# A hybrid attention block: the fourth query tile is turned in two transfers, and the rotary queries and mask biases are asked for at another place

## The chip, the cores and the metric

The kernel runs on one core of a Trainium2 chip. A core has the matrix engine PE (its weight loads, PEld, overlap its products), the vector engine DVE, the scalar engine ACT, the general engine POOL, and SP, which here computes nothing: it issues every DMA of the kernel, in one order, one after another. The metric is the time of one execution in microseconds (us). Three runs of the kernel before are shown, and beside them one profiled execution whose trace is read here.

## The reference

One decoder block: sixteen meta tokens stand ahead of 512 real ones, so L = 528 rows of width 1024, all in float32. Two attention branches run on one projection of the normalised input, and their gated outputs are added.

```python
u = rmsnorm(h, pre_norm_g)
cq, ckv, k_pe, z_mla, fq, fk, fv, f_logit, z_fox, gate_a, gate_b = split(u @ w_in)
# MLA: 16 heads; 64 plain and 32 rotary dimensions in queries and keys, values of 64
q = rmsnorm(cq) @ w_uq ; kv = rmsnorm(ckv) @ w_ukv
o_mla = causal_softmax_attention([q_nope, rope(q_pe)], [k_nope, rope(k_pe)], v_mla)
y_mla = (o_mla * silu(z_mla)) @ w_br_mla
# FoX: 16 heads of 64; a cumulative log forget gate is added to the scores
cum = cumsum(log_sigmoid(f_logit + b))
o_fox = causal_softmax_attention(fq, fk, fv, bias = cum[t] - cum[s])
y_fox = (o_fox * silu(z_fox)) @ w_br_fox
mixed = (sigmoid(gate_a) * y_mla + sigmoid(gate_b) * y_fox) @ w_out
return (h + rmsnorm(mixed, post_norm_g))[:, 16:]
```

## The kernel before

Products are split: an operand is kept as a high and a low 16-bit part, and one product becomes three (high x high, high x low, low x high), which is why PE does so much.

The attention runs as sixteen stages, `stages = [(br, pr) ...]`: for each pair of heads `pr` = 0..7 first FoX (`br` = 1), then MLA (`br` = 0). They are written (1,4), (0,4) and so on below. The 512 real queries are cut into four query tiles of 128, b = 0..3; tile b sees the meta keys and b+1 blocks of 128 keys, each block as a high and a low part, so 2b+3 tiles of probabilities for each of the two heads: 6, 10, 14 and 18 blocks of 128x128 for b = 0, 1, 2, 3.

One stage does this, each step with the name under which the profile shows it:

- `scores`: PE multiplies queries and keys into `st` (MLA's rotary part uses the tiles `KPH`, `KPL` and `QP`); DVE moves `st` to `sf` and adds a row of `cb` on the way (L1037). `cb` holds the forget-gate biases of the pair: plain ones, `cbp`, two loads of 264 KB by `bias` (L1159), and masked ones, `cbm`, made from them on POOL by `masked_bias`.
- ACT takes the exponential and sums each row into `su` (L1072). `norm(g)` then scales `su` (L1076) and inverts it into `ri` (L1077) in `inverse`, POOL does the meta columns (from L1092), ACT writes the high part of the normalised probabilities (L1107), DVE the low part (L1111), both into `pn`. Group g = 0 holds b = 0, 1, 2 (`pn0`), group 1 holds b = 3 (`pn1`).
- SP issues one DMA transpose for each query tile from `pn` into `ptt` (the profile's "pt<-pn"), at the end of `norm`. `ptt` has 18 blocks by 512 queries; tile b fills the first 2(2b+3) blocks of its own 128 queries.
- `values`: PE runs the 26 matmuls of `ov`: two on the meta block, then for each key block j = 0..3 six of them, which read blocks 2..5, 6..9, 10..13 and 14..17 of `ptt`. Their width shrinks with j: 512, 384, 256 and 128 queries. The two meta matmuls read block 0 and 1 of all four query tiles.

PE's order is written out by hand (`tc.manual_schedule`). Between a stage's scores and its `ov` stand the matmuls that project the next heads (`fq`, `fk`, `v`, `mq`, `mk`, `z`) and, right ahead of `ov`, the scores of the next stage. Each of these needs its weights: SP loads `wraw`, ACT, DVE and POOL (L274, L275) scale and split them into `w`. The order on DVE, ACT, POOL and SP is chosen by a scheduler from the program's order and priorities; `tc.issue_after(x)` adds that what it encloses stands behind x. SP carries all of it in one queue: weights `wraw`, transposes of values `vp<-vh`, biases `cbp`, transposes "pt<-pn", and for the rotary part of MLA's queries the stores to `qpe_dram` and the load `QP<-qpe_dram` of 256 KB. `load_qp` is called in `q_done`, when the pair's query projection has been evicted.

The DMAs use eight semaphores in turn, so that in the order below a DMA that names DMAHWn waits for the eighth one ahead of it, or for one whose bytes it needs. Names such as DVE or PE behind "waits" are the semaphores of the engines.

Of the kernel before, what the change touches and what calls it, by code (L numbers as in the profile page):

```python
# [17 lines left out]
ALU = mybir.AluOpType  # L18
# [8 lines left out]
NH = 16  # L27
# [13 lines left out]
PSCALE = 512.0  # L41
# [15 lines left out]
def block_kernel(ctx: ExitStack, tc: tile.TileContext, x, meta_tokens, pre_norm_g, w_in, fox_forget_b,  # L57
                 mla_q_norm_g, mla_kv_norm_g, w_uq, w_ukv, w_br_mla, w_br_fox, w_out, post_norm_g,
                 rope_tok, rope_pe, out):
    nc = tc.nc  # L60
# [21 lines left out]
    su = const.tile([128, 64], F32, tag="su", name="su")  # L82
# [12 lines left out]
    def dma(out, src, start=None):  # L95

        with tc.issue_after(sums_out[0]) if written[0] and sums_out else nullcontext():
            ins = (start or nc.sync.dma_start)(out=out, in_=src)
        if written[0]:
            tc.keep_in_program_order(ins)  # L100
        return ins.ins
# [683 lines left out]
    with ExitStack() as att:  # L785
# [38 lines left out]
        nc.gpsimd.memset(vh[:, 0], 0.0)  # L824
        for b in range(4):
            nc.gpsimd.memset(pn[b // 3][:, PN_STEP * b % 15], 0.0)
        gT = []
        masks, normed, whole, turned_p, between = [], [], [], [], []

        def load_qp(pr):  # L830
            dma(f32(QP), qpe_dram[2 * pr : 2 * pr + 2].rearrange("h i x f s -> (h i x f) s"))

        def q_mla(pr):
            def cuts(raw):
                return [(raw[:, 0:384].rearrange("p (b e) -> p b e", e=96)[:, :, 0:NOPE], lambda t: t[:, 0:256].rearrange("p (b e) -> p b e", e=NOPE)),
                        (raw[:, 384:640].rearrange("p (h a e) -> p a h e", h=2, a=2), lambda t: t[:, 256:512].rearrange("p (a h e) -> p a h e", a=2, h=2))]

            def wrap(w):
                mw[pr] = w
                return (lambda k: w[k][0]), (lambda k: w[k][1])  # L840
            get = mws[pr] = Parts(lambda: [wuq[:, :, 192 * pr : 192 * pr + 192], wukv[:, 256 * pr : 256 * pr + 256]], mla_room, cuts, wrap)

            halves = hl_done(("q", 0, pr), S, S, get)

            def q_done(i, ps):
                halves(i, ps)
                if pr:
                    load_qp(pr)
            return unit(f"mq{pr}", get, cq_act, 2, REAL, q_done)


# [144 lines left out]
        def attention(br, pr):  # L996
# [76 lines left out]
                                                                scale=-1.0, accum_out=sums["su"][:, h, b : b + 1]).ins  # L1073

            def inverse(su, ri):
                nc.vector.tensor_scalar(out=su, in0=su, scalar1=1.0 / PSCALE, scalar2=None, op0=ALU.mult)  # L1076
                return nc.vector.reciprocal(ri, su).ins  # L1077

            def norm(g):
                def fn():  # L1080
                    b0, nb_ = GRP[g][0], len(GRP[g])
                    su, ri = (sums[t][:, :, b0 : b0 + nb_] for t in ("su", "ri"))
                    if not (three_first and g):
                        inv = inverse(su, ri)
                    if three_first and g == 0:
                        with tc.issue_after(inv):
                            evict([p_ for p_ in places if p_[0] == 3])

                    mt = aw.tile([128, 2, nb_, META], F32, tag=f"mt{g}", name=f"mt{nm_}{g}", bufs=1)
                    src = sfs[g][:, :, 0 : SF_STEP * nb_].rearrange("p h (b c) -> p h b c", b=nb_)[:, :, :, 0:META]  # L1090
                    dst = pn[g][:, 0 : PN_STEP * nb_].rearrange("p (b t) h c -> p h b t c", b=nb_)[:, :, :, 0]
                    nc.gpsimd.tensor_tensor(out=mt, in0=src, in1=ri.unsqueeze(3).broadcast_to([128, 2, nb_, META]),  # L1092
                                            op=ALU.mult)
                    hi, lo, hi2 = (dst[:, :, :, 32 * i : 32 * i + META] for i in range(3))
                    nc.gpsimd.tensor_copy(hi, mt)
                    lead[:] = lead[-1:] + [nc.gpsimd.tensor_tensor(out=lo, in0=mt, in1=hi, op=ALU.subtract).ins]
                    nc.gpsimd.tensor_copy(hi2, mt)
                    def parts(b, h):
                        sf = sf_of(h, b)[:, META:].rearrange("p (j c) -> p j c", c=128)
                        t0 = PN_STEP * (b % 3) + 1  # L1100
                        hi, lo = (pn[g][:, t0 : t0 + 2 * b + 2, h].rearrange("p (j l) c -> p j l c", l=2)[:, :, i]
                                  for i in range(2))
                        return sf, hi, lo, sums["ri"][:, h, b : b + 1]

                    def high(b, h):
                        sf, hi, _, rib = parts(b, h)
                        normed[:] = [nc.scalar.activation(hi, sf, AF.Copy, scale=rib).ins]  # L1107

                    def lower(b, h):
                        sf, hi, lo, rib = parts(b, h)  # L1110
                        nc.vector.scalar_tensor_tensor(out=lo, in0=sf, scalar=rib, in1=hi, op0=ALU.mult, op1=ALU.subtract)  # L1111

                    early = three_first and g == 0
                    for b in GRP[g]:
                        if early and b == GRP[g][-1]:
                            for h in range(2):
                                high(b, h)
                            with tc.issue_after(normed[0]):
                                exponentials((3,))
                            inv = inverse(*(sums[t][:, :, 3:4] for t in ("su", "ri")))  # L1120
                            with tc.issue_after(inv):
                                for h in range(2):
                                    lower(b, h)
                            continue
                        for h in range(2):
                            high(b, h)
                            lower(b, h)
                    for b in GRP[g]:
                        t0, n = PN_STEP * (b % 3), 2 * b + 3
                        turned_p[:] = [dma(ptt[:, 0 : 2 * n, 128 * b : 128 * b + 128], pn[g][:, t0 : t0 + n].rearrange("p t h c -> p (t h c)"),  # L1130
                                           nc.sync.dma_start_transpose)]
                        if between and b == 1:
                            with tc.issue_after(turned_p[0]):
                                between.pop()()
                return fn
# [23 lines left out]
        def bias(pr):  # L1159

            return [nc.sync.dma_start(cb[0][h], c_dram[2 * pr + h : 2 * pr + h + 1].broadcast_to([128, L])).ins
                    for h in range(2)][1:]
# [35 lines left out]
        g = gate_unit(own=True)  # L1198
# [126 lines left out]
        for si, (br, pr) in enumerate(stages):  # L1325
# [4 lines left out]
            if br and si:  # L1330
                latent_first(sets[si - 1][2], halved[("k", 1, pr), 1])
            sc()
            for fn in late:
                fn()
            if si == 0:
# [24 lines left out]
            else:  # L1360
# [10 lines left out]
                if si == 2:  # L1371
                    behind.clear()
                n0()
                if pr and not (br or last):
                    bias(pr + 1)
                if br:
                    sets[si][0].scale()
                for job in middles[si]:
# [410 lines left out]
```

## Time and profile before

| | |
|---|---|
| three runs | 585.48, 585.65, 582.69 us (median 585.48) |
| the profiled execution | 582.32 us, its span 580.5 us |
| granted clock of PE | 0.998 |
| PE busy | 559.7 us, 96% of the span |
| DVE, ACT, POOL busy | 471.0 (81%), 407.5 (70%), 240.3 us (41%) |
| the chain that ended last | PE 74%, DVE 12%, ACT 5%, issue 3%, DMA 3% |
| transposes pt<-pn | 64 (four in each of the sixteen stages) |
| DMA queue q1 | 97.03 MB, 70.1% of 16 engines' span |

"Busy" adds up an engine's instructions; the chain is followed back from the last instruction to what released each one, and says which engine's work lay on the way to the end. An idle stretch of PE is printed with what released it; where that says "issue", the profile shows nothing that the engine waited for, though the program's order may still show a wait. The span is 1.8 us shorter than the execution's own time, and that execution is 0.5% below the median of the three runs.

### The profile page before, as it was taken

What the parts mean: (1) busy time and instruction counts of PE and PEld (TensorE: products, weight loads), DVE (VectorE), ACT (ScalarE), POOL (GpSimd) and SP (SyncE); (2) the same over time, 40 slices, a digit from 0 to 9 for tenths busy, and PEclk for the clock granted to TensorE, in tenths of its full rate; (3) what the DMA queues carried; (4) which work ended last, traced back from release to release, by engine and by line L of the source; (5) the groups of instructions that cost most, each with busy time, mean ns of one, the idle gap of its engine ahead of it and who ended that gap; (6) DMA issues with size and microseconds to landing.
All of it is one profiled execution on the core that took longest, in us unless ns stands there. A gap on an engine that the chain in (4) does not pass through costs nothing.

```text
span 580.5 us, 11367 instructions
## 1 busy us (share of the span) xinstructions
PE 559.7 (96%) x3865; PEld 391.6 (67%) x3865; DVE 471.0 (81%) x1255; ACT 407.5 (70%) x891; POOL 240.3 (41%) x361
## 2 busy tenths in 40 slices
PE   7999979999899999989999999999999999999995
PEld 6888647667567568557566675645776675788884
DVE  5878899887877988887877879879958986478966
ACT  7869679788887887878887988964443463343762
POOL 4422723785783897866847857700000000000000
PEclk9999999999999999999999999999999999999999
DMA  8625789889999697998995984668924230333603
GB/s 286 147 65 152 216 176 280 177 191 250 190 231 202 159 194 144 221 204 163 262 228 119 237 199 121 139 146 278 299 76 109 73 110 6 110 104 108 218 1 145
DMA packets 220026, 97.75 MB, mean 168 GB/s; under 512 B 131352, under 2 KB 209568, under 8 KB 219968
## 3 DMA queue, kind: packets, MB, share of 16 engines
q1 hardware_dynamic: 219968, 97.03, 70.1%
q8 instruction: 30, 0.49, 0.3%
q14 instruction: 28, 0.23, 0.1%
HBM read 62.62 MB, written 4.23 MB: 115 GB/s over the span
## 4 chain that ended last, share of the span: by engine, by line
PE 74%; DVE 12%; ACT 5%; issue 3%; DMA 3%; POOL 1%; SPq 1%; DVEq 0%; ACTq 0%; POOLq 0%
PE z L104 16%; PE pg L104 10%; PE py L104 8%; PE st L104 6%; PE fq L104 6%; PE x L104 6%; PE v L104 6%; PE ov L104 5%; PE fk L104 5%; PE psm L104 2%; PE y L104 2%; PE mq L104 2%; DVE w L272 2%; DVE sc L204 1%; DVE wl L110 1%
## 5 line engine op out<-in xcount | busy, mean ns | idle before, releaser
L104 PEld LDWEIGHTS <-w 128*128 128x128 f16 x1752 | 168.2, 98 | 126.4 <-DVE w L272 2.5
L1072 ACT ACTIVATE sf<-sf,nb 128x272 f32<-128x272 f32 (+3 forms) x128 | 72.7, 569 | 21.2 <-DVE nb L1037 19.6
L104 PE MATMUL z<-hTh,w 128*128 128x512 f16 x256 | 81.6, 379 | 0.3 <-DVE w L272 0.3
L220 POOL TENSOR_SCALAR sc<-sc,su 128x3 f32<-128x3 f32 (+3 forms) x23 | 9.9, 432 | 163.8 <-DVE sc L217 163.8
L275 POOL TENSOR_TENSOR w<-wraw,w 128x1024 f16<-128x1024 f32 x35 | 75.2, 2148 | 2.3
L1111 DVE SCALAR_TENSOR_TENSOR pn<-sf,ri,pn 128x512 f16<-128x512 f32 (+3 forms) x128 | 70.9, 612 | 3.5 <-ACT pn L1107 3.5
L104 PE MATMUL pg<-hTh,w 128*128 128x512 f16 x240 | 72.6, 379 | 0.8 <-DVE w L272 0.8
L1107 ACT ACTIVATE pn<-sf,ri 128x128 f16<-128x128 f32 (+3 forms) x128 | 59.6, 547 | 6.0 <-issue 2.3
L261 ACT ACTIVATE w<-wraw,sc 128x1024 f16<-128x1024 f32 x42 | 47.0, 1142 | 11.3 <-DVE sc L219 9.0
L110 DVE TENSOR_TENSOR wl<-wraw,w 128x512 fp32r<-128x512 f32 (+1 forms) x44 | 38.5, 881 | 12.5 <-PE scale L104 4.4
L104 PE MATMUL z<-hTl,w 128*128 128x512 f16 x128 | 48.5, 379 | 0.0
L274 POOL TENSOR_SCALAR wraw<-wraw,sc 128x1024 f32<-128x1024 f32 x35 | 39.7, 1133 | 15.3 <-ACT w L261 14.5
L104 PE MATMUL pg<-hTl,w 128*128 128x512 f16 x120 | 45.5, 379 | 0.0
L104 PE MATMUL st<-hlk,hlq 64*128 64x240 f32 (+4 forms) x480 | 42.4, 300 | 1.2 <-DVE gT L894 0.9
L104 PE MATMUL fk<-hTh,w 128*128 128x272 f16 (+1 forms) x224 | 40.2, 276 | 0.0
L104 PE MATMUL ov<-pt,vp 128*64 128x512 f16 (+4 forms) x416 | 32.6, 306 | 6.9 <-DMA pt<-pn 3.4
L104 PEld LDWEIGHTS st<-hlk,hlq 64*128 64x128 f32 x480 | 33.6, 186 | 8.2 <-ACT vh L961 1.7
L104 PE MATMUL v<-hTh,w 128*128 128x272 f16 (+1 forms) x224 | 39.1, 276 | 0.0
L202 ACT ACTIVATE junk<-wraw 128x1024 bf16<-128x1024 f32 (+2 forms) x35 | 33.7, 964 | 3.8 <-DMA wraw<-in_w_in_dram 3.5
L104 PEld LDWEIGHTS <-vp 128*64 128x64 f16 (+1 forms) x416 | 22.6, 109 | 19.3 <-issue 11.6
L104 PE MATMUL fq<-hTh,w 128*128 128x512 f16 x112 | 34.5, 380 | 0.0
L1492 ACT CAST w<-wraw 128x512 fp32r<-128x512 f32 x28 | 16.8, 617 | 23.0 <-DVE wraw L1501 18.5
(345 smaller groups left out, 1459.5 us busy)
## 6 DMA issues: line engine op xcount, KB each, us to landing
wraw<-in_w_in_dram SPq DMA_DIRECT2D x46, 512.0 KB
room<-in_w_in_dram SPq DMA_DIRECT2D x9, 512.0 KB
cbp<-c_dram SPq DMA_DIRECT2D x16, 264.0 KB
wraw<-in_w_br_fox_dram SPq DMA_DIRECT2D x8, 512.0 KB
tb<-in_w_out_dram SPq DMA_DIRECT2D x8, 512.0 KB
wraw<-in_w_br_mla_dram SPq DMA_DIRECT2D x8, 512.0 KB
wraw<-in_w_out_dram SPq DMA_DIRECT2D x6, 512.0 KB
QP<-qpe_dram SPq DMA_DIRECT2D x8, 256.0 KB
```

The source lines that it names most:

```text
L104: nc.tensor.matmul(*a, **k)
L110: return eng.tensor_tensor(out=lo, in0=src, in1=f32(hi), op=ALU.subtract)
L202: tc.keep_in_program_order(nc.scalar.activation(junk[0][:, 0:n], raw, AF.Abs, accum_out=mp))
L220: nc.gpsimd.tensor_scalar(out=r, in0=t, scalar1=su[:, 5:6], scalar2=1.0, op0=ALU.mult, op1=ALU.mult)
L261: self.hi = nc.scalar.activation(hi, raw, AF.Copy, scale=self.s).ins
L272: nc.vector.scalar_tensor_tensor(out=lo, in0=raw, scalar=self.s, in1=hi, op0=ALU.mult, op1=ALU.subtract)
L274: nc.gpsimd.tensor_scalar(out=raw, in0=raw, scalar1=self.s, scalar2=1.0, op0=ALU.mult, op1=ALU.mult)
L275: nc.gpsimd.tensor_tensor(out=lo, in0=raw, in1=hi, op=ALU.subtract)
L1072: exps[b // 3] = nc.scalar.activation(sf, sf, AF.Exp, bias=sums["nb"][:, h, b : b + 1], scale=-1.0, accum_out=sums["su"][:, h, b : b + 1]).ins
L1107: normed[:] = [nc.scalar.activation(hi, sf, AF.Copy, scale=rib).ins]
L1111: nc.vector.scalar_tensor_tensor(out=lo, in0=sf, scalar=rib, in1=hi, op0=ALU.mult, op1=ALU.subtract)
L1492: nc.scalar.copy(to[0], src)
```

## The change

Three edits. First, the transpose of query tile b = 3 goes out as two DMAs: tiles 0 to 4 (10 blocks: meta, j = 0, j = 1) and tiles 5 to 8 (8 blocks: j = 2, j = 3). Second, in `inverse` the sums are scaled through a view whose two outer dimensions are exchanged. Third, for pairs 1 to 6 the call `bias(pr + 1)` moves from the MLA stage (0,pr), behind `n0()`, to the FoX stage (1,pr), right behind `sc()`; its second DMA is kept in `biased`, and `load_qp` of the pair is issued behind it.

```diff
@@ load_qp, q_done
-        gT = []
+        gT, biased = [], []
...
                 if pr:
-                    load_qp(pr)
+                    with tc.issue_after(biased[0]) if biased else nullcontext():
+                        load_qp(pr)
+                    biased.clear()
@@ inverse
-                nc.vector.tensor_scalar(out=su, in0=su, scalar1=1.0 / PSCALE, scalar2=None, op0=ALU.mult)
+                su_ = su.rearrange("p h b -> p b h")
+                nc.vector.tensor_scalar(out=su_, in0=su_, scalar1=1.0 / PSCALE, scalar2=None, op0=ALU.mult)
@@ norm
-                        turned_p[:] = [dma(ptt[:, 0 : 2 * n, 128 * b : 128 * b + 128], pn[g][:, t0 : t0 + n].rearrange("p t h c -> p (t h c)"),
-                                           nc.sync.dma_start_transpose)]
+                        for t, m in ((0, 5), (5, 4)) if b == 3 else ((0, n),):
+                            turned_p[:] = [dma(ptt[:, 2 * t : 2 * (t + m), 128 * b : 128 * b + 128],
+                                               pn[g][:, t0 + t : t0 + t + m].rearrange("p t h c -> p (t h c)"), nc.sync.dma_start_transpose)]
@@ the loop over stages
             sc()
+            if br and 1 <= pr < NH // 2 - 1:
+                biased[:] = bias(pr + 1)
...
                 n0()
-                if pr and not (br or last):
-                    bias(pr + 1)
```

On PE, ACT and POOL the order of the instructions is the same in both kernels, and on DVE too, but for the form of the scaling (128x2x3 becomes 128x3x2 where the group has three query tiles; the form 128x2 of the fourth stays). SP's queue changes, and with it what PE waits for.

SP's queue in the FoX stage (1,4), before: the last transpose of stage (0,3), two stores of rotary queries, the load of QP which waits for both of them, weights, the biases, and this stage's transposes of 6, 10, 14 and 18 blocks.

```order
L98 DMA_TRANSPOSE pt<-pn_777 128x14x128 [waits DMAHW2_49,DVE_49]
L98 DMA qpe_dram<-gT_1016 2x16x512 [waits DMAHW3_49,Pool_49]
L98 DMA qpe_dram<-gT_1016 2x16x512 [waits DMAHW4_49,Pool_49]
L98 DMA QP<-qpe_dram 128x512 [waits DMAHW5_49,DMAHW4_49,DMAHW3_49]
L98 DMA wraw_3747<-in_w_in_dram 128x8x128 [waits DMAHW6_49,Pool_49]
L98 DMA_TRANSPOSE vp_782<-vh 128x9x128 [waits DMAHW7_49,DVE_49]
L98 DMA wraw_3749<-in_w_uq_dram 128x2x192 [waits DMAHW0_49,Activation_49,Pool_49]
L98 DMA wraw_3749<-in_w_ukv_dram 128x256 [waits DMAHW1_49]
L98 DMA wraw_4183<-in_w_in_dram 128x8x128 [waits DMAHW2_49,Pool_49]
L1161 DMA cbp_767<-c_dram 128x528 [waits DVE_49]
L1161 DMA cbp_766<-c_dram 128x528 [waits DVE_49]
L98 DMA_TRANSPOSE pt<-pn_777 128x6x128 [waits DVE_49,DMAHW5_49,PE_49,Pool_49]
```

The same stretch of SP's queue after, from the weights behind the stores to the end of the stage's transposes.

```order
L98 DMA wraw_3756<-in_w_in_dram 128x8x128 [waits DMAHW5_49,Pool_49]
L98 DMA_TRANSPOSE vp_782<-vh 128x9x128 [waits DMAHW6_49,DVE_49]
L98 DMA wraw_3758<-in_w_uq_dram 128x2x192 [waits DMAHW7_49,Activation_49,Pool_49]
L98 DMA wraw_3758<-in_w_ukv_dram 128x256 [waits DMAHW0_49]
L98 DMA wraw_4196<-in_w_in_dram 128x8x128 [waits DMAHW1_49,Pool_49]
L1165 DMA cbp_767<-c_dram 128x528 [waits DMAHW2_49,DVE_49]
L1165 DMA cbp_766<-c_dram 128x528 [waits DMAHW3_49,DVE_49]
L98 DMA QP<-qpe_dram 128x512 [waits DMAHW4_49]
L98 DMA_TRANSPOSE pt<-pn_777 128x6x128 [waits DVE_49,DMAHW5_49,PE_49,Pool_49]
L98 DMA_TRANSPOSE pt<-pn_777 128x10x128 [waits DMAHW6_49,DVE_49,PE_49]
L98 DMA_TRANSPOSE pt<-pn_777 128x14x128 [waits DMAHW7_49,DVE_49,PE_49]
L98 DMA_TRANSPOSE pt<-pn_778 128x10x128 [waits DMAHW0_49,DVE_49]
```

The load of QP has moved from ahead of the weights to behind the biases, directly ahead of the stage's transposes; the biases stand where they stood. The transpose of 18 blocks is now one of 10, and one of 8 follows it. The same holds in (1,5). In stages (1,1), (1,2), (1,3) and (1,6) the load of QP comes to the same place behind the biases, from the MLA stage ahead, where it stood directly before the four transposes.

SP's queue in the MLA stage (0,1), before: QP of the next pair, and the four transposes, in which the fourth query tile comes second.

```order
L98 DMA wraw_2373<-in_w_in_dram 128x8x128 [waits DMAHW7_49,Pool_49]
L98 DMA QP<-qpe_dram 128x512 [waits DMAHW1_49,DMAHW0_49,PE_49]
L98 DMA_TRANSPOSE pt<-pn_777 128x6x128 [waits DVE_49,PE_49,Pool_49]
L98 DMA_TRANSPOSE pt<-pn_778 128x18x128 [waits DMAHW2_49,DVE_49,PE_49]
L98 DMA_TRANSPOSE pt<-pn_777 128x10x128 [waits DMAHW3_49,DVE_49]
L98 DMA_TRANSPOSE pt<-pn_777 128x14x128 [waits DMAHW4_49,DVE_49]
```

And after.

```order
L98 DMA wraw_2380<-in_w_in_dram 128x8x128 [waits DMAHW2_49,Pool_49]
L98 DMA_TRANSPOSE pt<-pn_777 128x6x128 [waits DVE_49,DMAHW3_49,PE_49,Pool_49]
L98 DMA_TRANSPOSE pt<-pn_778 128x10x128 [waits DMAHW4_49,DVE_49,PE_49]
L98 DMA_TRANSPOSE pt<-pn_777 128x10x128 [waits DMAHW5_49,DVE_49]
L98 DMA_TRANSPOSE pt<-pn_777 128x14x128 [waits DMAHW6_49,DVE_49,PE_49]
L98 DMA_TRANSPOSE pt<-pn_778 128x8x128 [waits DMAHW7_49,PE_49]
```

Ahead of this stage's transposes no QP stands any more, and the second half of the fourth tile comes last, behind the 14 blocks of the third.

PE at the start of `ov` in stage (1,4), before: behind the last scores, the first weight load waits for four DMAs, the stage's four transposes.

```order
L104 MATMUL st_3653<-KPH,QP 128x400
L104 MATMUL st_3654<-KPH,QP 128x400
L104 MATMUL st_3653<-KPL,QP 128x400
L104 MATMUL st_3654<-KPL,QP 128x400
L104 LDWEIGHTS vp_782 [waits DMAHW5_49,DMAHW6_49,DMAHW0_49,DMAHW7_49]
L104 MATMUL ov_3675<-pt,vp_782 64x512 [waits PE_49]
```

After, the first weight load still waits for four DMAs, now with the 10-block half among them, and the wait for the 8-block half stands fourteen matmuls later, at the first one of j = 2.

```order
L104 LDWEIGHTS vp_782
L104 MATMUL ov_3686<-pt,vp_782 64x384
L104 LDWEIGHTS vp_782
L104 MATMUL ov_3686<-pt,vp_782 64x384
L104 LDWEIGHTS vp_782
L104 MATMUL ov_3686<-pt,vp_782 64x256 [waits DMAHW1_49]
```

One wait of `ov` has become two, the second of them behind the two meta matmuls and the twelve of j = 0 and j = 1.

## The prediction

> **What bounds the kernel now.** I read the page first, for the engine that fills the span and the chain.
>
> ```profile
> span 580.5 us, 11367 instructions
> PE 559.7 (96%) x3865; PEld 391.6 (67%) x3865; DVE 471.0 (81%) x1255; ACT 407.5 (70%) x891; POOL 240.3 (41%) x361
> ...
> PE 74%; DVE 12%; ACT 5%; issue 3%; DMA 3%; POOL 1%; SPq 1%; DVEq 0%; ACTq 0%; POOLq 0%
> ...
> L104 PE MATMUL ov<-pt,vp 128*64 128x512 f16 (+4 forms) x416 | 32.6, 306 | 6.9 <-DMA pt<-pn 3.4
> ```
>
> PE is busy for 559.7 of 580.5 us, so a change that alters no PE work can win only what PE idles. The last row gives the size of the matter: in all sixteen stages together PE idles 6.9 us ahead of `ov`, 1.2% of the span. The change touches just the DMAs for which `ov` waits. The view of waits, for PE, names what ended that idle time, and what ended the idle time of the scores.
>
> ```profile
> PE ov L104 <- DMA pt<-pn: 3.4, 2, 1.8
> PE ov L104 <- issue: 3.1, 2, 2.0
> ...
> PE st L104 <- DVE gT L894: 0.9, 1, 0.9
> ...
> PE ov L104 <- PE st L104: 0.3, 1, 0.3
> ```
>
> Each row is: engine and tile waiting, releaser, total us, times, longest. So `ov` waits visibly in five of sixteen stages. "issue" is no cause; the order shows that the weight load ahead of that `ov` waits for the four transposes. PE's timeline places the five, the idle time in brackets; the row at 189.44 is the wait for L894, the one at 369.48 an `ov` that did not wait, and the one at 252.31 belongs to the `ov` of 251.28, its six matmuls of j = 1.
>
> ```profile
> 87.09 1.22 PE L104 MATMUL ov<-pt,vp 80*64 80x512 f16 x10 [1.82 <-DMA pt<-pn]
> 148.59 1.65 PE L104 MATMUL ov<-pt,vp 80*64 80x512 f16 x16 [1.58 <-DMA pt<-pn]
> 189.44 2.25 PE L104 MATMUL st<-hlk,hlq 64*128 64x272 f32 x29 [0.93 <-DVE gT L894]
> 251.28 2.04 PE L104 MATMUL ov<-pt,vp 80*64 80x512 f16 x26 [1.99 <-issue]
> 252.31 0.63 PE L104 MATMUL ov<-pt,vp 128*64 128x384 f16 x6
> 291.37 1.87 PE L104 MATMUL ov<-pt,vp 80*64 80x512 f16 x20 [1.12 <-issue]
> 330.58 1.65 PE L104 MATMUL ov<-pt,vp 80*64 80x512 f16 x16 [0.25 <-PE st L104]
> 369.48 1.22 PE L104 MATMUL ov<-pt,vp 80*64 80x512 f16 x10
> ```
>
> The stages are (1,0), (0,1), (1,4), (1,5), (1,6) and, for 369.48, (1,7). Their idle times add up to 1.82 + 1.58 + 1.99 + 1.12 + 0.25 = 6.76 us.
>
> **What delays the transposes there.** SP's timeline for (1,4), (1,5), (1,6) and (1,7), and its waits; columns are start, length, what and how many. Rows of one transpose alone stand below the four that they belong to.
>
> ```profile
> 226.32 1.54 SPq L98 DMA_DIRECT2D qpe_dram<-gT  x2
> 232.13 0.35 SPq L98 DMA_DIRECT2D QP<-qpe_dram  x1
> ...
> 236.55 0.38 SPq L98 DMA_DIRECT2D wraw<-in_w_in_dram  x1
> 236.98 1.06 SPq L1161 DMA_DIRECT2D cbp<-c_dram  x2
> 239.90 9.12 SPq L98 DMA_TRANSPOSE pt<-pn  x4
> ...
> 245.29 3.73 SPq L98 DMA_TRANSPOSE pt<-pn  x1
> ...
> 280.08 9.27 SPq L98 DMA_TRANSPOSE pt<-pn  x4
> ...
> 286.05 3.30 SPq L98 DMA_TRANSPOSE pt<-pn  x1
> ...
> 316.92 1.01 SPq L1161 DMA_DIRECT2D cbp<-c_dram  x2
> 320.16 8.43 SPq L98 DMA_TRANSPOSE pt<-pn  x4
> ...
> 359.37 7.83 SPq L98 DMA_TRANSPOSE pt<-pn  x4
> ...
> SPq L98 <- DMA qpe_dram<-gT: 8.6, 2, 4.4
> ```
>
> The stores' issue ends at 227.86, and QP goes out at 232.13: SP stands still for over 4 us until the stores have landed, once in (1,4) and once in (1,5), 8.6 us together. Everything behind in the queue, four weight loads and a transpose of values among it, then comes in one heap ahead of this stage's transposes. The windows show the heap, the DMA share second to last and GB/s last in each row:
>
> ```profile
> 228.00:233.00 5.00, 5.00 (x62) 3.59 (x61) 4.67 (x27) 4.00 (x14) 4.82 (x7) 1.00 0.36 93
> 233.00:252.00 19.00, 17.01 (x124) 9.94 (x124) 17.00 (x59) 16.20 (x38) 16.16 (x19) 1.00 1.09 219
> ...
> 364.40:366.50 2.10, 2.10 (x16) 1.09 (x16) 1.24 (x7) 1.90 (x5) 2.02 (x3) 1.00 1.14 209
> 366.60:369.10 2.50, 2.50 (x42) 2.50 (x42) 2.50 (x10) 1.31 (x4) 2.50 (x3) 1.00 1.04 181
> ```
>
> The DMA engines are at 0.36 while SP stands still, and full (1.09) from then until `ov` starts. The last two rows are the ends of the 14- and 18-block transposes in (1,7): full engines, 181 to 209 GB/s.
>
> **The change part by part.** I go against the profiled execution, 582.32 us, which is 3.16 us under the median of 585.48; the differences are carried over to the median at the end.
>
> *The split.* A block is 128 x 128 x 2 bytes, 32.8 KB, so 8 blocks are 262 KB. `ov` no longer waits for these: at 181 to 209 GB/s that is 1.25 to 1.45 us of transfer taken from in front of it. Its lower end is zero or worse (rival 3). I take 1.25, the faster row, since the engines have to finish the first half as they would the whole. The 8-block half is wanted by j = 2, which starts some 1.4 us after `ov` (252.31 + 0.63 = 252.94 is the end of the last j = 1 matmul, and `ov` started at 251.28; a matmul overlaps the next by some 0.2). Its transfer, 1.25 to 1.45, ends about then, so a second wait of 0 to 0.3 us may be left. On SP the issue of one 18-block transpose takes 3.30 and 3.73 us in the limited stages, as long as the engines are full; two issues of the smallest kind seen, 1209 ns each in the group of pt<-pn, are shorter than that, so SP's sixteen more DMAs cost nothing there.
>
> ```profile
> L98 SPq DMA_TRANSPOSE pt<-pn x64: 1209/1614/3977, 74.5 to 381.9; - x64
> ```
>
> *QP behind the biases.* In (1,4) and (1,5) SP is freed of 4.2 and 4.4 us. The weights behind the stores go out into engines that are 64% idle. What is gained for the transposes is bounded by rows: (1,6) has the same queue without that wait, biases directly ahead, and its four take 8.43 us to issue, 0.7 to 0.8 less than 9.12 and 9.27. Against it stands QP's own load, now directly ahead of the transposes: 256 KB, 1.25 us at 209 GB/s if the engines are full by then, and 0.35 us of SP. In (1,4) the issue fits in the stretch from 238.04 to 239.90 in which SP waits anyway. So for the transposes this part lies between +0.5 (1.25 - 0.75) and -0.8; I take -0.45. In (1,1), (1,2), (1,3), (1,6) QP comes where SP has a stretch as well: in (1,6) from 317.93 to 320.16. What covers it is SP's wait ahead of the first transpose; if that wait were gone, each would cost 0.35 us of SP. What needs QP is late enough: the first scores with QP in (1,4) start at 246.2 (next fence), 8 us behind the biases.
>
> ```profile
> L104 PE MATMUL st<-KPH,QP x10: 271/283/346, 246.2 to 248.8; 64*128 64x272 f32 x2, 64*128 64x240 f32 x2, 64*128 64x144 f32 x2, 64*128 64x288 f32 x2
> ...
> 136.18 0.58 SPq L98 DMA_DIRECT2D QP<-qpe_dram  x1
> 136.87 8.34 SPq L98 DMA_TRANSPOSE pt<-pn  x4
> ```
>
> The last two rows are stage (0,1): there QP leaves from directly ahead of the transposes, which could start 0.69 us earlier.
>
> *The biases.* The order puts their two DMAs at the same place of SP's queue: 0.
>
> *The form of the scaling.* DVE's 32 scalings take 142 to 1658 ns. The long ones are not the reshaped form: the rows below show a 128x2 scaling at 234.52 that ends at 236.18, when POOL's L275 ends (236.15).
>
> ```profile
> 234.52 1.66 DVE L1076 TENSOR_SCALAR su<-su 128x2 f32<-128x2 f32 x1
> ...
> 234.02 2.13 POOL L275 TENSOR_TENSOR w<-wraw,w 128x1024 f16<-128x1024 f32 x1
> ```
>
> The 128x2 form stays as it is, so this is 0; between 142 ns each saved and lost, sixteen of them off PE's path.
>
> *The sum, stage by stage.* (1,4): 1.25 + 0.45 = -1.70 of 1.99. (1,5): the split alone covers the 1.12; I take -1.1. (1,6): its 0.25, I take -0.2. (0,1): split and QP, 1.25 + 0.69, exceed 1.58; but whatever PE wins before 189 us meets the 0.93 us wait for L894, a chain of DVE work that does not follow from `ov`: PE that comes earlier waits longer there. I take -0.2 out of 1.58. (1,0): 1.82 lies before the same wait, 0. Sum: -1.7 - 1.1 - 0.2 - 0.2 = -3.2 us. The ends: 0, if PE's earlier arrival is given back everywhere, and -6.76, if all is won. So 582.32 becomes 579.1, and the median 585.48 becomes 582.3, -0.55%.
>
> **Rivals.** *1. Given back, no change.* DVE has 17.00 busy of 19 us in 233 to 252 and POOL 16.16, so the engines behind PE have about 2 us of room per stage; with QP in front of six FoX stages' transposes at up to 1.25 us of transfer, the first half lands no earlier than the whole did before. For it: the 1.09 share. Against: QP's bytes move in every version, only earlier, and the stall on stores wastes engines. It gives -1 to +1, 585. A change that does not do what it says belongs here too: the order shows the biases not moved at all.
>
> *2. All `ov` waits go.* It needs the L894 wait to follow. For it: the 0.69 us that leave stage (0,1). It gives up to 585.48 - 6.76, 578.7; I put it at 580.
>
> *3. Slower: the two halves do not overlap.* Between the end of the 18-block issue and `ov` lie 291.37 - 289.35 = 2.02 us and 251.28 - 249.02 = 2.26 us. If a second transfer could begin only when the first has landed, it would be 1.21 + 2.02 = 3.2 us behind it; with the first 1.25 earlier and j = 2 1.4 later, `ov` would end 0.6 us later than now. It decides once the halves land more than 2.65 us apart. Over the six FoX stages (1,1) to (1,6), which I count as without room, that is +3.6 us: 589.1, +0.6%. Against it: in (1,7) the four are issued within 7.83 us, and `ov` starts, unwaited, 10.1 us after the first issue began; four in series would need 4 x 3.2 = 12.8.
> The Trainium skill speaks for this rival: its page "DMA: Bandwidth & Descriptors" (Anatomy of one DMA; Rules for kernel authors) gives each DMA about 2.0 us of fixed cost and asks for many small transfers to be merged into a large one. By its fit, as an estimate, 18 blocks would take 3.35 us and 10 and 8 blocks 2.75 + 2.60, 2.0 more in each stage; the overlap in (1,7) does not bear out that the fixed parts add up one behind another.
>
> **How the numbers follow.** Forecast (1.5 to 4.5 us won) 0.50; rival 1, 0.26; rival 2, 0.12; rival 3, 0.12. A measurement here tells about 0.5%, 2.9 us, from no change. The forecast's own range is 581 to 584; its centre of 3.2 is just past that line, so about two thirds of it count as faster: 0.33 + 0.12 = 0.45 faster, 0.17 + 0.26 = 0.43 within, 0.12 slower. The range: the lower end is the gain of 6.76 with one more us for medians (the three runs alone lie 3 us apart), 577.7; the upper end is rival 1's +1, 586.5. Rival 3 is left out.
>
> **What would show it.** In the changed kernel's profile: no stretch of SP over 4 us behind the stores of rotary queries in (1,4) and (1,5); PE's idle time ahead of the first `ov` matmul in these stages under 0.4 and 0.1 us; at the first 256-wide matmul of j = 2 no new idle time above 0.3; the total at `ov` down from 6.9 to about 3; the wait for L894 grown from 0.9 by about what (0,1) has lost. I am wrong if j = 2 waits for more than its half of what the first half won, if the scores with QP wait for its load, or if DVE or POOL releases a new PE wait after 251 us.

## The result, and the profile after

The changed kernel takes 578.72 us (median of 5 runs, 578.01 to 579.4), the kernel before 582.94 us in the runs beside it (5 runs, 582.6 to 585.65). The ratio is 0.9918, with a 95% interval of 0.9899 to 0.9937: 0.8% faster. The profiled execution of the changed kernel took 578.01 us, that of the kernel before 582.32.

The page of the changed kernel, the rows that answer to those shown before the change:

```profile
span 576.2 us, 11400 instructions
PE 560.6 (97%) x3865; PEld 391.1 (68%) x3865; DVE 471.4 (82%) x1255; ACT 407.5 (71%) x891; POOL 240.3 (42%) x361
...
L104 PE MATMUL ov<-pt,vp 128*64 128x512 f16 (+4 forms) x416 | 32.8, 307 | 2.2 <-DMA pt<-pn 2.1
```

The work of the engines is nearly as before (PE 560.6 us against 559.7); the idle time of PE ahead of `ov` has gone from 6.9 to 2.2 us. PE's timeline shows where the rest of it lies, in brackets:

```profile
84.93 0.84 PE L104 MATMUL ov<-pt,vp 80*64 80x512 f16 x6 [0.50 <-DMA pt<-pn]
146.90 0.84 PE L104 MATMUL ov<-pt,vp 80*64 80x512 f16 x6 [0.91 <-DMA pt<-pn]
187.69 0.52 PE L104 MATMUL st<-hlk,hlq 64*128 64x272 f32 x4 [0.93 <-DVE gT L896]
247.72 1.54 PE L104 MATMUL ov<-pt,vp 80*64 80x512 f16 x14
249.99 0.52 PE L104 MATMUL ov<-pt,vp 128*64 128x256 f16 x6 [0.72 <-DMA pt<-pn]
287.71 1.06 PE L104 MATMUL ov<-pt,vp 80*64 80x512 f16 x8
326.62 1.05 PE L104 MATMUL ov<-pt,vp 80*64 80x512 f16 x8
```

Stage (1,4) starts its `ov` without a wait and runs fourteen matmuls; then it waits 0.72 us at the first 256-wide matmul of j = 2, where the 8-block half is wanted. (1,5) and (1,6) have no wait that the timeline prints. The wait for L896 (the line that was L894) is 0.93 us, as it was.

SP's timeline of the changed kernel in (1,4), and two single transposes out of the five:

```profile
225.17 1.29 SPq L98 DMA_DIRECT2D qpe_dram<-gT  x2
228.36 0.38 SPq L98 DMA_DIRECT2D wraw<-in_w_in_dram  x1
228.84 2.01 SPq L98 DMA_TRANSPOSE vp<-vh  x1
...
234.89 1.01 SPq L1165 DMA_DIRECT2D cbp<-c_dram  x2
235.95 0.42 SPq L98 DMA_DIRECT2D QP<-qpe_dram  x1
238.14 9.34 SPq L98 DMA_TRANSPOSE pt<-pn  x5
...
243.25 2.87 SPq L98 DMA_TRANSPOSE pt<-pn  x1
...
246.22 1.26 SPq L98 DMA_TRANSPOSE pt<-pn  x1
```

Behind the stores SP's next DMA, a load of weights, now goes out at 228.36, after 1.9 us; before, it was the load of QP, after 4.3 us. No row of SP's waits names the stores any more. The 10-block half goes out at 243.25; its issue takes 2.87 us, so the 8-block half goes out only at 246.22, 2.97 us behind it. For 1.25 us of that issue the DMA engines move next to nothing (the granted clock of PE, the engines' busy share and GB/s are the last three columns):

```profile
243.50:244.75 1.25, 1.25 (x12) 0.71 (x12) 0.66 (x4) 0.92 (x3) 1.17 (x2) 1.00 0.05 5
```

In (1,5), whose transposes have no such pause, the two halves go out 1.94 us apart, and `ov` has no second wait:

```profile
283.49 1.84 SPq L98 DMA_TRANSPOSE pt<-pn  x1
...
285.43 1.36 SPq L98 DMA_TRANSPOSE pt<-pn  x1
```

So the 0.72 us wait at j = 2 goes with the late issue of the 8-block half, and that with the pause, to which the last section comes back.

### The profile page after: what moved, and what is told of

The parts are those of the page before. It is cut to its first block, busy times and chain, and to the rows that moved or that the text cites. A ratio compares the mean times of both kernels' runs of the same rounds, so it can differ in the third digit from the quotient of the medians.

```text
span 576.2 us, 11400 instructions
## 1 busy us (share of the span) xinstructions
PE 560.6 (97%) x3865; PEld 391.1 (68%) x3865; DVE 471.4 (82%) x1255; ACT 407.5 (71%) x891; POOL 240.3 (42%) x361
## 3 DMA queue, kind: packets, MB, share of 16 engines
HBM read 62.62 MB, written 4.23 MB: 116 GB/s over the span
## 4 chain that ended last, share of the span: by engine, by line
PE 70%; DVE 12%; DMA 5%; ACT 5%; issue 3%; POOL 3%; SPq 0%; DVEq 0%; POOLq 0%; ACTq 0%
PE z L104 14%; PE pg L104 10%; PE py L104 8%; PE x L104 6%; PE fq L104 5%; PE v L104 5%; PE st L104 5%; PE ov L104 4%; PE fk L104 4%; DMA pt<-pn 3%; PE psm L104 2%; PE y L104 2%; DVE w L272 1%; DMA wraw<-in_w_in_dram 1%; PE mq L104 1%
## 5 line engine op out<-in xcount | busy, mean ns | idle before, releaser
L275 POOL TENSOR_TENSOR w<-wraw,w 128x1024 f16<-128x1024 f32 x35 | 75.1, 2146 | 2.3
L202 ACT ACTIVATE junk<-wraw 128x1024 bf16<-128x1024 f32 (+2 forms) x35 | 33.7, 964 | 3.4 <-DMA wraw<-in_w_in_dram 3.0
```

What stands on the lines that cost most here:

```text
L202: tc.keep_in_program_order(nc.scalar.activation(junk[0][:, 0:n], raw, AF.Abs, accum_out=mp))
L275: nc.gpsimd.tensor_tensor(out=lo, in0=raw, in1=hi, op=ALU.subtract)
```

## The experiments

All times are device us; a ratio is to runs of the kernel before on the same chip. The table collects what each kernel measured, and the idle time of PE in the stages that matter, ahead of `ov` (a second number, behind a +, is inside `ov`), from the timelines. A wait under 0.15 us, which the timeline does not print, is a difference of its rows. One profiled execution stands behind each row, and such executions differ by up to 0.7 us in a stage, as the first two rows show, which are the same program but for the form of a scaling; a smaller difference in one stage shows nothing by itself. Nor is the profiled execution always a middling one: that of the split alone (583.29 us) is the slowest of its twelve, that of the scaling alone (585.22) the second slowest, that of the moves for pairs 4 and 5 alone (581.03) the fastest.

| kernel | median | ratio (95%) | (0,1) | (1,4) | (1,5) | (1,6) |
|---|---|---|---|---|---|---|
| before | 582.94 to 583.69 | 1 | 1.58 | 1.99 | 1.12 | 0.25 |
| scaling alone | 583.60 | 1.0005 (0.9991 to 1.0018) | 1.67 | 1.81 | 1.60 | 0.95 |
| moves alone | 583.59 | 1.0012 (0.9994 to 1.0029) | 1.22 | 0.98 | 1.26 | 1.38 |
| moves for pairs 4, 5 alone | 582.76 | 0.9985 (0.9968 to 1.0003) | 1.40 | 1.76 | 0 | 0.96 |
| no QP loads, no split | 581.59 | 0.9966 (0.9952 to 0.9981) | 1.33 | 1.12 | 0.65 | 0.54 |
| split alone | 581.80 | 0.9969 (0.9955 to 0.9982) | 0.92 | 1.32 | 1.91 | 0 |
| split, moves for pairs 1, 2, 3, 6 | 580.35 | 0.9937 (0.9915 to 0.9959) | 0.92 | 0.32 + 0.68 | 1.80 | 0 |
| split, moves for pairs 4, 5 | 578.95 | 0.9922 (0.9905 to 0.9938) | 1.02 | 0.69 | 0.21 | 0 |
| the whole change | 578.72 | 0.9918 (0.9899 to 0.9937) | 0.91 | 0 + 0.72 | 0.12 | 0 |
| the change, no QP loads | 578.21 | 0.9920 (0.9901 to 0.9940) | 0.61 | 0.36 | 0 | 0 |
| the change, cut 14 and 4 | 581.41 | 0.9956 (0.9939 to 0.9973) | 1.01 | 0.72 | 1.67 | 0.52 |
| the change, last blocks first | 581.47 | 0.9977 (0.9959 to 0.9996) | 0.65 + 0.35 | 0.52 + 0.95 | 0.04 + 0.65 | 0 + 0.13 |
| the change, third tile cut too | 586.30 | 1.0041 (1.0024 to 1.0058) | 1.46 + 0.59 | 0 + 0.94 | 0.82 + 2.21 | 0 |

### The three edits by themselves

**The split alone.**

```diff
-                        turned_p[:] = [dma(ptt[:, 0 : 2 * n, ...
+                        for t, m in ((0, 5), (5, 4)) if b == 3 else ((0, n),):
+                            turned_p[:] = [dma(ptt[:, 2 * t : 2 * (t + m), ...
```

> Before, with the split of the fourth query tile's transpose alone; QP, biases and the scaling stay. Theory A (the gain is the sum of waits taken from ahead of ov): the first ov waits for 262 KB less, so (1,4) loses about 0.5 to 1.2 of its 1.99 us, (1,5) its 1.12, (1,6) its 0.25, (0,1) about 0.7 of 1.58, and SP still stands still for over 4 us behind the stores in (1,4) and (1,5): 2.0 to 3.2 us faster than before. Rival R1 (the stall of SP behind the stores is what mattered): at most 1 us faster. Rival R3 (halves do not overlap): a wait above 0.6 us at j = 2 in most stages, slower.

It measured 0.3% faster, 1.7 us: under the 2.0 that Theory A gave at least, and over R1's 1, though the interval (1.1 to 2.6 us) reaches into Theory A's range. The halves do overlap: no wait stands inside any `ov`. But (1,5) waits 1.91 us, longer than before, and SP's rows show a part of why. SP's wait for the stores in this kernel (total, times, longest):

```profile
SPq L98 <- DMA qpe_dram<-gT: 8.6, 2, 4.4
```

Its timeline of SP from the end of stage (0,4) on:

```profile
266.66 1.86 SPq L98 DMA_TRANSPOSE pt<-pn  x1
268.57 1.48 SPq L98 DMA_DIRECT2D qpe_dram<-gT  x2
274.47 0.36 SPq L98 DMA_DIRECT2D QP<-qpe_dram  x1
...
280.37 10.12 SPq L98 DMA_TRANSPOSE pt<-pn  x5
```

And PE's `ov` of (0,4) and (1,5):

```profile
270.79 1.93 PE L104 MATMUL ov<-pt,vp 80*64 80x512 f16 x22
...
291.40 3.23 PE L104 MATMUL ov<-pt,vp 80*64 80x512 f16 x26 [1.91 <-DMA pt<-pn]
```

The 3.23 us of the second row, where an `ov` takes 2.04 elsewhere, hold no second wait. PE's clock was granted at 0.50 for 3.41 us there, which costs this execution some 1.7 us, an estimate:

```profile
292.07:295.48 3.41, 3.41 (x25) 2.25 (x22) 1.33 (x6) 2.78 (x8) 2.31 (x9) 0.50 1.06 305
```

So the missing wait in (1,6), which comes behind it, shows nothing of the split. The wait of 1.91 us came ahead of that stretch. The stores of rotary queries stand behind stage (0,4)'s transposes, which are five now, so they leave at 268.57, where they left at 267.71 before. QP waits for them until 274.47 (before: 273.84), and everything up to the transposes of (1,5) follows in a row: they start at 280.37, against 280.08 before, while PE is 0.75 us earlier (`ov` of (0,4) at 270.79, against 271.54). The start of the transposes hangs on the stall, not on PE, and the split has lengthened the queue ahead of the stall. That is not all. `ov` starts 4.23 us after the issue of the 10-block half began (at 287.17), where it started 5.32 us after that of the 18-block transpose began (at 286.05 before): the split wins 1.1 us here too. But the half's issue began 1.1 us later than the whole's had. 0.3 us of this are the later start, 0.7 us a longer issue of the second tile's 10 blocks, 3.63 us in place of 2.91; why that took longer stays open.

**The moves alone** (the biases and `load_qp` as in the diff of the change, without its other two edits).

> Before, with the moved biases and rotary queries alone; the fourth tile is turned in one transfer of 18 blocks, the scaling as before. Theory A: SP no longer stands still behind the stores; (1,4) loses 0.5 to 1 of its wait, (1,5) 0.5 to 1.1, (0,1) about 0.7 through the QP that leaves: 1.0 to 2.5 us faster. R1: 3 us or more faster, as much as the whole change.

No difference: 1.0012. Theory A's 1.0 to 2.5 us did not come, and R1 is out. The stall is gone here too, and (1,4) waits 0.98 us in place of 1.99, as expected; but (1,5) keeps its wait and (1,6) waits 1.38 us, where it waited 0.25 before (and 0.95 with the scaling alone). The rows of PE for (1,4), (1,5) and (1,6):

```profile
250.59 2.04 PE L104 MATMUL ov<-pt,vp 80*64 80x512 f16 x26 [0.98 <-PE st L104]
...
290.83 2.04 PE L104 MATMUL ov<-pt,vp 80*64 80x512 f16 x26 [1.26 <-issue]
...
331.17 2.04 PE L104 MATMUL ov<-pt,vp 80*64 80x512 f16 x26 [1.38 <-DMA pt<-pn]
```

**The form of the scaling alone** (`su_ = su.rearrange("p h b -> p b h")` in `inverse`).

> Before, with the exchanged dimensions of the scaled sums alone. Theory A: no difference that can be measured (within 0.3 us in the median of several runs), and the 0.84 us by which the changed kernel was ahead before its first transpose comes and goes between executions of kernels that do not differ there. Rival R2 (the scaling counts): 0.5 us or more, with shorter scalings in the group of L1076.

No difference: 1.0005. The 32 scalings take 145 to 1674 ns here, 142 to 1658 before, and the rows of lines give 11.4 us for all of them in the changed kernel, 11.2 before. R2 is out. The start of the first transpose, 75.1 us here, 74.5 before and 73.7 in the changed kernel, does come and go.

### Which loads of QP matter, and where the moves' gain went

**The whole change, but the rotary queries behind the biases for pairs 4 and 5 only.**

```diff
-                    with tc.issue_after(biased[0]) if biased else nullcontext():
+                    with tc.issue_after(biased[0]) if biased and pr in (4, 5) else nullcontext():
```

> The changed kernel, with the rotary queries behind the biases for pairs 4 and 5 only; for pairs 1, 2, 3 and 6 they stay in the MLA stage ahead. Theory A: the stalls of SP are gone as in the changed kernel, so (1,4) and (1,5) gain as there; (0,1) loses the part that QP's leaving gave, 0.3 to 0.7 us: 0 to 0.7 us slower than the changed kernel, 3 to 4 us faster than before. Rival: QP ahead of the FoX transposes costs in (1,1), (1,2), (1,3) and (1,6), then this kernel is faster than the changed one.

0.9922: as fast as the whole change, and 4.5 us faster than before. Theory A holds for (1,4) and (1,5); what QP's leaving would have given in (0,1) is 0.1 us (1.02 against 0.91), less than put down. The rival, that this kernel is the faster one, is not borne out.

**The reverse: for pairs 1, 2, 3 and 6 only** (`pr not in (4, 5)`).

> The changed kernel, with the rotary queries behind the biases for pairs 1, 2, 3 and 6 only; for pairs 4 and 5 they stay behind the stores, so SP stands still there as before. Theory A (split and stall interact: the stall fixes when the transposes of (1,4) and (1,5) leave, and the split, which lengthens SP's queue ahead of the stores, cannot win there): like the split alone, 1 to 2.5 us faster than before, with waits of over 1 us at ov in (1,4) and (1,5). Rival (the pairs 1, 2, 3 and 6 carry the gain): 3.5 us or more faster.

0.9937, 3.3 us faster, more than Theory A's 2.5 and less than the rival's 3.5. The place that tells them apart speaks for Theory A: with the stall, (1,5) waits 1.80 us, as with the split alone. (1,4) waits for less than with the split alone, 0.32 + 0.68. How the remaining gain comes about stays open; the intervals of this kernel and of the split alone overlap.

**The moves for pairs 4 and 5, without the split.**

> Before, with the rotary queries behind the biases for pairs 4 and 5 only, no split, the scaling as before. Theory A (ahead of unsplit transposes QP costs in (1,1) and (1,6) what the end of the stall wins in (1,4)): 0.8 to 1.8 us faster than before, with (1,4) at about 1 us and (1,6) at 0 to 0.9 us of wait. Rival (the end of the stall wins nothing without the split, whatever QP does elsewhere): within 0.4 us of before.

0.9985: between Theory A and the rival, and by the interval not told from before. In its trace, of the fastest of twelve executions, (1,4) waits 1.76 us, where Theory A had about 1, (1,5) not at all, and (1,6) 0.96. That the next stage takes what one stage wins is a guess: with the scaling alone (1,6) waits as long.

**No loads of QP at all for pairs 1 to 6**, in the kernel before and in the changed one (`if pr == 7: load_qp(pr)`).

> Before, without the loads of the rotary queries of pairs 1 to 6 (the MLA scores of these pairs use those of pair 0): no QP bytes, no stall behind the stores, fourth tile in one transfer. It bounds from above what any place of these loads can win in the unsplit kernel. Theory B (an unsplit FoX stage has no room, so the pauses of the DMA engines and the remaining loads keep its waits): at most 1 us faster than before. Rival (the moves win nothing because QP costs ahead of the FoX transposes what the stall's end wins): 2 us or more faster.

> The changed kernel, without the loads of the rotary queries of pairs 1 to 6 (as above). It bounds what a still better place of QP could win beside the split. Theory B (with the split, QP ahead of the FoX transposes is covered): within 0.5 us of the changed kernel. Rival (QP ahead of the transposes still costs): 1 us or more faster than the changed kernel.

Without the split the missing loads give 0.9966, 1.4 us by the medians: between Theory B's 1 us and the rival's 2. Against the moves alone (1.0012) it is 0.46% less, with intervals that do not touch, so the loads of QP do cost something beside unsplit transposes, as rival 1 had said; whether their place or their bytes cost it is not told apart. But six `ov` still wait, for 5.2 us together, without any of these loads and any stall. With the split the missing loads give nothing that can be measured (0.9920 against 0.9918): there QP is covered. The rows of waits of the first and of the second:

```profile
PE ov L104 <- DMA pt<-pn: 5.2, 6, 1.4
```

```profile
PE ov L104 <- DMA pt<-pn: 1.6, 3, 0.6
```

### What makes the split pay

**The key blocks of `ov` in the order 3, 2, 1, 0**, so that both halves are needed at once.

```diff
-                for j in range(4):
+                for j in (3, 2, 1, 0):
...
-                               stop=(j == 3 and i == 2))
+                               stop=(j == 0 and i == 2))
```

> The changed kernel, with the key blocks of ov taken in the order j = 3, 2, 1, 0, so that the third matmul of ov already needs the 8-block half: two transfers, but nearly nothing runs between the two waits. Theory A (the split wins only because fourteen matmuls run while the second half is under way): the split's part is lost, (1,4), (1,5) and (0,1) wait about 1.2 us longer than in the changed kernel, 581.5 to 583.5 us. Rival (two shorter transfers land earlier by themselves, or the moves carry the gain): within 1 us of the changed kernel.

581.47 us: 2.7 us of the changed kernel's gain are lost, a hair under Theory A's 581.5. The waits come back inside `ov`, in this kernel's rows behind the two meta matmuls, at the first 128-wide matmul:

```profile
249.11 0.41 PE L104 MATMUL ov<-pt,vp 80*64 80x512 f16 x2 [0.52 <-PE st L104]
250.46 1.82 PE L104 MATMUL ov<-pt,vp 128*64 128x128 f16 x24 [0.95 <-DMA pt<-pn]
...
290.31 1.82 PE L104 MATMUL ov<-pt,vp 128*64 128x128 f16 x24 [0.65 <-DMA pt<-pn]
```

Against the changed kernel the waits of (1,4), (1,5) and (0,1) are longer by 0.75, 0.57 and 0.09 us, less than the 1.2 expected of each; that of (1,0) is longer by 0.41. So most of the gain hangs on the matmuls between the two waits. Not all of it does: this kernel is still 0.2% faster than before, and where that comes from is not shown.

**The fourth tile cut into 14 and 4 blocks** (`((0, 7), (7, 2))`).

> The changed kernel, with the fourth tile cut into 14 and 4 blocks in place of 10 and 8. Theory A (what stands ahead of ov counts by its blocks): the first part lands 0.4 to 0.7 us later in each limited stage, (0,1) and (1,4) wait that much longer ahead of ov, and no wait is left inside ov: 0.3 to 1.5 us slower than the changed kernel. Rival (only the number of transfers counts, or the last one's landing): the same as the changed kernel.

2.7 us slower than the changed kernel by the medians, more than the 0.3 to 1.5 expected; the direction is Theory A's. (1,4) waits 0.72 ahead of `ov`, with nothing inside; (1,5) 1.67 and (1,6) 0.52, where four blocks less had left almost nothing. So the first part's size counts; why four blocks cost 1.5 us in (1,5), more than the 0.7 us that they take at 181 GB/s, stays open.

**The third tile cut too**, 10 and 4 blocks, the 4 sent behind the first half of the fourth tile.

> The changed kernel, with the third tile cut too, 10 and 4 blocks, the 4 sent behind the first half of the fourth tile: 32 DMAs more than before in place of 16. Theory A: four blocks less ahead of ov, 0.4 to 0.7 us off the wait in (0,1), about as much given back at j = 2 in (1,4): 0 to 0.7 us faster than the changed kernel. Rival R3 (each transfer has a price of its own): slower than the changed kernel by 1 us or more.

Slower than before by 0.4%, and 7.6 us slower than the changed kernel by the medians. R3's forecast is right here, where it was wrong for the one cut. The rows of the transposes, of this kernel and then of the changed one (shortest, median and longest issue in ns, first and last start):

```profile
L98 SPq DMA_TRANSPOSE pt<-pn x96: 1211/1360/3085, 74.7 to 388.6; - x96
```

```profile
L98 SPq DMA_TRANSPOSE pt<-pn x80: 1211/1550/3675, 73.7 to 378.6; - x80
```

Two of PE's waits in this kernel:

```profile
PE ov L104 <- DMA pt<-pn: 4.6, 4, 2.2
PE scale L104 <- ACT junk L202: 2.4, 4, 0.8
```

And its `ov` of (1,5):

```profile
292.55 1.54 PE L104 MATMUL ov<-pt,vp 80*64 80x512 f16 x14 [0.82 <-DMA pt<-pn]
296.30 1.04 PE L104 MATMUL ov<-pt,vp 128*64 128x256 f16 x12 [2.21 <-DMA pt<-pn]
```

No issue here is shorter than 1211 ns, whatever the size, and half of the 96 take over 1360. Six of them in a stage cost SP at least 7.3 us, five 6.1. The second half of the fourth tile is now the sixth, and `ov` waits 2.21 us for it in (1,5); the waits of `scale` for L202, which reads the weights, have grown from 0.6 to 2.4 us. R3's reason is not shown to be the cause: the cut also puts four blocks of the third tile behind the first half of the fourth, and a third cut in the old order was not tried. In this execution, too, the granted clock was 0.50 for 3.41 us, from 296.48 on.

## Why the prediction was right, and which steps failed

**Direction and size.** The forecast was 582.3 us, -0.55%, against a median of 585.48; measured is 578.72 against 582.94, -0.8%, and the interval (-0.6 to -1.0%) does not hold -0.55%. The reason was right: what the traces show of the gain comes from waits ahead of `ov`. The median of the three runs shown lay high: the later runs of the kernel before have medians of 582.94 to 583.69. One term is missing from the sum: PE's granted clock. It was 0.996 or less in 30 of 78 executions of the kernel before that stand beside the experiments, and in one of 17 of the whole change and of the two kernels that equal it in time (QP behind the biases for pairs 4 and 5 only, and no loads of QP). Span times what the clock lacks is 1.7 to 2.1 us on average before and 1.0 to 1.4 us in these three. So some 0.7 us of the 4.2 us between the medians, an estimate, may be the clock's; why it goes with the change is not shown.

**The sum by stages**, the profiled executions compared. PE is 0.8 us ahead when the first transposes leave (74.5 against 73.7 us), before anything changed can act: the kernel before waits 1.18 us for POOL (L484) at 9.47 us, this execution of the changed kernel does not, and the six kernels that were made from the changed one do (0.66 to 1.44 us). That part is no effect of the change. From there to the end of the last `ov` 3.1 us are won, where the sum had 3.2, and the last 0.3 of the 4.3 us between the two spans lie behind it. So the sum is right, but not its terms; that they add up is luck, since what (1,4) won less (0,1) won more.

- (1,4): -1.70 forecast, -1.1 measured. 1.99 us ahead of `ov` are gone, and 0.72 stand at j = 2, where I had put 0 to 0.3: I took the second half to land 1.25 to 1.45 us behind the first, but its issue came 2.97 us after the first one's, 1.25 of them in the pause. I had read the engines as full from 233 us until `ov` starts; their mean share of 1.09 hid a like pause in the kernel before (245.25 to 246.50), inside the issue of the 18 blocks whose 3.73 us I put down to full engines.
- (1,5): -1.1 forecast, -1.0 measured, but for another reason. "The split alone covers the 1.12" is wrong: the split alone leaves 1.91. This is the step that failed: I added the terms as if each landed by itself. Split -0.3%, moves 0, both -0.8%: the times show that most of the gain takes the end of the stall and the split together. For (1,5) alone the traces do not agree: the moves alone leave 1.26 us there, the moves for pairs 4 and 5 alone none.
- QP behind the biases: -0.45 for the transposes, by itself worth nothing over the whole kernel. Rival 1's mechanism, QP ahead of unsplit FoX transposes, fits this (1.0012 with these loads, 0.9966 without them); the split covers it.
- (1,6): -0.2 forecast, -0.3 measured, within what executions differ by.
- (0,1): -0.2 forecast, -0.7 measured. The split and QP were to exceed its 1.58 us, and 0.91 us of it are left. I had said that PE, coming earlier, would wait longer for L894. It waits 0.93 us in the kernel before and in the changed one: the DVE work there follows PE, so a gain from before it is kept.
- (1,0): 0 forecast. Its wait fell from 1.82 to 0.50, and most of that was given back ahead of the next `ov`, which starts 22.1 us after it (107.01 - 84.93), 21.0 before (108.04 - 87.09): -0.2 in all. So PE that comes earlier does wait longer here, though not for L894: the new waits are for ACT, 0.34 us for L202 and 0.65 for L425.
- The scaling's form and the biases' place: 0 forecast. The first shows no difference; the second was only tried together with QP.

**Rival 2**, that all `ov` waits go, had a time as near as the forecast's: up to 578.7 us, and 578.72 came. It is not what happened: 2.1 of the 6.76 us at `ov` are left. Its condition, that the wait for L894 follows PE, did hold. Of the signs that I named, two failed: j = 2 waits for more than 0.3 us in (1,4), and the wait for L894 has not grown.

**Rival 3**, that the two halves do not overlap: wrong for this cut. Only (1,4) has a second wait, and its 0.72 us are less than the 1.99 us won ahead of it. With the third tile cut too, (1,5) waits 0.82 and 2.21 us, where it waited 1.12 before. The rule of the Trainium skill that stood beside it ("DMA: Bandwidth & Descriptors", Rules for kernel authors: merge many small transfers into a large one) agrees with that last kernel and not with the changed one: 16 transfers more cost PE nothing that shows, and the next 16, with the new order, 7.6 us by the medians. The 2.0 us for each transfer, from which the prediction's estimate came, stand in the Trainium skill ("DMA: Bandwidth & Descriptors", Anatomy of one DMA) for DMAs that GpSimd issues; SP issues these.

## What to carry to other kernels

A transfer that a chain of matmuls waits for can be cut where the matmuls' own order needs it later. The cut pays if there is work between the two waits: with the key blocks in reverse order most of the gain was lost. One cut more was a loss here, for a reason that is not settled. Terms that share a queue are not added one by one: ask for each what the transfers' start hangs on. Here neither the end of a fixed stall nor the split gave by itself what they gave together. Test edits apart and together before believing in either.

## What the runs showed that was not expected

The DMA engines have pauses that no row of waits names. The view of DMA queues for 239 to 249 us, in forty slices of 0.25 us, of the kernel before:

```profile
DMA  8999999999999974999999999300009999990999
GB/s 244 287 328 301 273 308 339 392 378 381 329 297 301 206 108 92 268 270 215 259 282 198 328 259 89 4 1 8 9 10 227 290 289 313 267 114 9 258 201 284
...
q8 instruction: 1, 0.02, 0.7%
```

and of the changed kernel:

```profile
DMA  9999999934999999990000079999999961999982
GB/s 268 342 349 314 347 270 174 97 35 82 276 290 290 288 282 261 283 88 0 0 6 9 9 160 293 291 290 277 290 291 290 290 138 28 211 211 212 203 171 71
...
q8 instruction: 1, 0.02, 0.6%
```

In the midst of stage (1,4)'s transposes the engines move 0 to 10 GB/s for five slices, 1.25 us, in both kernels, while transposes are being issued. In each window lies one packet of 0.02 MB on the instruction queue. The other two stages of the changed kernel that still wait at `ov` have a packet and a pause as well, shortly ahead of the `ov` that starts at 84.93 and the one at 146.90:

```profile
83.00:84.50 1.50, 1.43 (x18) 1.09 (x15) 1.15 (x2) 1.45 (x2) 0.00 (x0) 1.00 0.04 4
145.15:146.40 1.25, 0.84 (x12) 0.50 (x8) 1.18 (x8) 0.61 (x2) 1.12 (x2) 1.00 0.12 6
```

So the three waits that are left each come behind a pause. All thirteen traces have a packet and a pause of some 0.9 to 1.6 us in (1,4), and none has either in (1,5). But in (0,4) a packet lies among the transposes in all thirteen, and only one of them has such a pause there. That the packet makes the pause is not shown, only that they often come together. The Trainium skill, "Runtime: NRT & Kernel Launch" (Instruction fetch mechanics), says that instructions are fetched in blocks of 16 KiB by a DMA queue and that the cost is mostly hidden; the size agrees with the packet. If the fetch is what stops the engines, its cost is hidden here only in stages whose transposes have room for the pause; no run here moves or removes a packet, so that stays open.

PE's clock has stretches of its own. Besides the one at the end of each, three of the thirteen profiled executions have one of 3.41 us at a granted clock of 0.50: the split alone, the scaling alone (from 149.56) and the third tile cut too. Each begins 0.2 to 0.7 us after PE took up an `ov` for which it had waited 1.67 to 2.21 us. Waits of 1.82 and 1.99 us in the kernel before have no such stretch behind them, so a long wait does not always bring one. If the two are linked, a wait removed saves more than its own length now and then.
